# Weights' casts and one head's scaling on GpSimd in the attention steps, and weight loads ordered behind the queries' transfers

## The chip, the core and the metric

The kernel runs on one core of a Trainium2 chip. A core has a matrix engine (TensorE: PE in the profile, with its weight loads shown apart as PEld), VectorE (DVE), ScalarE (ACT), GpSimd (POOL) and SyncE (SP), which here only issues DMAs. The engines run side by side, each through its own list of instructions in a fixed order, and wait for one another by semaphores. The metric is the device time of one execution in microseconds (us); three executions of the kernel before took 1140.64, 1141.03 and 1141.64 us.

## The reference

A two-layer decoder trunk on 512 tokens of width 1024, in float32: a gated mixer, a gated MLP with a short convolution and a gated per-layer embedding in layer 0; then one shared K/V; then, in layer 1, sliding-window attention, and the MLP and embedding again. The change lies in layer 1's attention:

```python
q = (xn @ w_q).reshape(B, nb, BLOCK, N_KV_HEADS, GQA_GROUP, HEAD_DIM)
scores = einsum('bnikgd,bnjkd->bnkgij', q, kblk) * HEAD_DIM ** -0.5
scores = where(valid, scores - slopes * dist, -inf)
m = maximum(max(scores, -1), sink)
e = exp(scores - m)
probs = e / (sum(e, -1) + exp(sink - m))
out = einsum('bnkgij,bnjkd->bnikgd', probs, vblk)
return out.reshape(B, S, N_Q_HEADS * HEAD_DIM) @ w_o
```

There are 16 query heads of 64 in 4 groups, which share a K/V head each, and 4 blocks of 128 tokens; each block sees itself and the block before.

## The kernel before

**Products.** Every float32 operand is split into a high part, rounded to the matrix engine's format `fp32r`, and a remainder. A product is three matmuls: high by high, high by remainder, remainder by high (`mm3`, lines 181 to 183). For a weight the split is done on the way: `load` (line 122) fetches a piece of up to 2048 columns into a raw buffer with one DMA on SP's queue (line 129); `pump` (line 133) takes a unit of up to 1024 columns of it, casts it to the high part `wh` (line 154, on ACT) and subtracts for the remainder `wl` (line 155, on DVE). Four `wh` and four `wl` buffers exist (`WBUFS`). A piece is loaded when its first unit is pumped, so the loops' order is also that of the loads. `chunk` takes the units that a product needs and pumps some ahead.

**The attention steps** (line 864). `steps` holds 16 pairs (group, block), blocks innermost. Turn `i` of the loop calls
- `scores(i)`: eight matmuls of queries by keys (lines 781, 782), and on DVE the choice of the half that is valid (784) and distance, mask and row minimum in one (788); a copy of the sink logits on POOL (774); four exponentials with their sums on ACT (793);
- `fill(i)`: matmuls and casts from the table `beside`, which stand between the attention's own: projections of the queries of groups 1 to 3 (`project`), the first parts of the output projection (`merge`), and `more`, which pumps one unit of weights. `more` stands in steps 0, 1, 3, 4, 6, 7, 10 and 11;
- `mix(i-2)`: probabilities by values (844), and on ACT, DVE and POOL the results' way into the operands of the output projection (848 to 857);
- `turn(i-1)`: four transposes on PE (822), the split of the result (252 on ACT, 253 on DVE), and for blocks with a predecessor two selects on POOL (830);
- `weights(i)`: a reciprocal of the four sums on DVE (801), and each head's probabilities by it: three heads on ACT (805), the first on DVE (807).

In the loop the raw weights have one buffer only (`state["tags"] = [0]`), since the others hold transposed probabilities and values. `queries` (line 641) scales a projection and splits it, and for groups 1 to 3 brings both parts into place with four DMAs on SP's queue (661, 662).

**The order of each engine's list** is made by a planner when the program is built: it goes by the order of the loops, moves `scores`, `turn` and `weights` forward (`tc.high_priority()`), and lets an instruction pass others that are not ready by its own estimates of durations. A change of one instruction's engine can so move others.

The profile names tiles without their numbers: `wraw`, `wh` and `wl` are weights, `sc` scores, `prs` probabilities, `tr` their transposes, `pts` and `u` their split, `pv` values' products, `o` output projection, `oh` and `ol` its operands.

Of the kernel before, what the change touches and what calls it, by code (L numbers as in the profile page):

```python
# [8 lines left out]
F32 = mybir.dt.float32  # L9
# [4 lines left out]
P = 128  # L14
# [34 lines left out]
def tile_yoco(ctx: ExitStack, tc: tile.TileContext, t, out: bass.AP, out_b: bass.AP):  # L49
    nc = tc.nc  # L50
# [14 lines left out]
    pieces, paired = [], set()  # L65
# [51 lines left out]

    units = [(i, q, lo, n) for i, p in enumerate(pieces) for q, (lo, n) in enumerate(p[2])]
    raws, ready = {}, {}
    state = {"raw": 0, "unit": 0, "next": 0, "tags": [0, 1, 2], "turn": 0, "pt": 0}  # L120

    def load(upto, queue=nc.sync):
        while state["raw"] < min(upto, len(pieces)):
            j = state["raw"]
            a, m = pieces[j][:2]
            tags = state["tags"]
            r = wp.tile([P, 2 * UNIT], F32, tag=f"r{tags[state['turn'] % len(tags)]}", bufs=1, name=f"wraw{j}")
            state["turn"] += 1
            queue.dma_start(r[:, :m].rearrange("p (c m) -> p c m", c=2) if j in paired else r[:, :m], a)
            raws[j] = r  # L130
            state["raw"] += 1

    def pump(upto):
        while state["unit"] < min(upto, len(units)):
            i, q, lo, n = units[state["unit"]]
            load(i + 1)
            u = state["unit"]
            own = pieces[i][3]
            if own:
                pool, *tags = own[q]  # L140
                wh, wl = (pool.tile([P, n], F32R, tag=tg, name=f"own{u}_{tg}") for tg in tags)
            else:
                wh = wp.tile([P, UNIT], F32R, tag="wh", bufs=WBUFS, name=f"wh{u}")
                wl = wp.tile([P, UNIT], F32R, tag="wl", bufs=WBUFS, name=f"wl{u}")
            if i in paired:
                whole = raws[i][:, : pieces[i][1]].rearrange("p (c k n) -> p k c n", c=2, n=256)
                src = whole[:, lo // S : (lo + n) // S]
                hi, low = (x[:, :n].rearrange("p (k c n) -> p k c n", c=2, n=256) for x in (wh, wl))
            else:
                src, hi, low = raws[i][:, lo : lo + n], wh[:, :n], wl[:, :n]  # L150
            if u == 0:
                nc.vector.tensor_copy(hi, src)
            else:
                nc.scalar.copy(hi, src)  # L154
            nc.vector.tensor_sub(low, src, hi.bitcast(F32))  # L155
            ready[u] = (wh, wl, n)
            state["unit"] += 1
# [41 lines left out]
    def v(name, i):  # L199
        c = VEC[name] + i  # L200
        return vec[:, c : c + 1]
# [142 lines left out]
    def gain(name, l=0):  # L344
        return lambda k: v(name, l * KD + k)
# [215 lines left out]
    for c in range(4):  # L561
# [4 lines left out]
        for j in range(2):  # L566
            m = 2 * c + j
# [14 lines left out]
            hi = ap.tile([P, S], F32R, tag=f"ah{m}", name=f"ush{m}")  # L582
# [58 lines left out]
    def queries(ps, g, j):  # L641


        qf = tp.tile([P, S], F32, tag="sq", name=f"qf{g}_{j}")
        m = 2 * g + j
        nc.vector.scalar_tensor_tensor(qf, ps, qscale[:, m : m + 1], rstd, op0=ALU.mult, op1=ALU.mult)
        res = [tp.tile([P, S], F32R, tag=("hs", "sg", "c0", "c1")[2 * j + e], name=f"q{g}_{j}_{e}")
               for e in range(2)]
        if g == 0:
            for e, q in enumerate(res):  # L650
                me, it = sides[e], sides[1 - e]
                nc.scalar.copy(q[me, :], qf[me, :])
                nc.vector.tensor_sub(q[it, :], qf[me, :], q[me, :].bitcast(F32))
            return res

        hi = tp.tile([P, S], F32, tag="acc", name=f"qhi{g}_{j}")
        nc.scalar.copy(hi.bitcast(F32R), qf)
        nc.vector.tensor_sub(qf.bitcast(F32R), qf, hi)
        for e, q in enumerate(res):
            me, it = sides[e], sides[1 - e]  # L660
            nc.sync.dma_start(q[me, :].bitcast(F32), hi[me, :])
            nc.sync.dma_start(q[it, :].bitcast(F32), qf[me, :])
        return res

    qs = {0: []}
    for j in range(2):
        qs[0] += queries(qps[j], 0, j)
# [61 lines left out]
    def more():  # L729

        pump(state["unit"] + 1)
# [23 lines left out]
    def fill(i):  # L755
        for f, *args in beside.get(i, []):
            f(*args)
# [9 lines left out]
    def scores(i):  # L767


        g, n = steps[i]  # L770
        nk = 2 * P if n else P
        t0 = (n - 1) * P if n else 0
        pr = prs[:, i % 2]
        nc.gpsimd.tensor_copy(pr[:, :, P], nsink[:, GQ * g : GQ * (g + 1)])
        neg = at.tile([P, GQ], F32, tag="neg", bufs=2, name=f"neg{i}")
        for b in range(2):
            sc = psum(f"sc{i}_{b}").rearrange("p (e h k) -> p e h k", e=2, h=2)
            for j in range(2):
                o = sc[:, j].rearrange("p h k -> p (h k)")[:, :nk]
                q = qs[g][2 * b + j][:, n * P : (n + 1) * P]  # L780
                nc.tensor.matmul(o, q, kh[g // 2][:, g % 2, t0 : t0 + nk], start=True, stop=False)
                nc.tensor.matmul(o, q, kl[g // 2][:, g % 2, t0 : t0 + nk], start=False, stop=True)
            if n:
                nc.vector.copy_predicated(sc[:, :, 0, :], both(own.bitcast(mybir.dt.int32)), sc[:, :, 1, :])
            for j in range(2):
                e = 2 * b + j
                hd = GQ * g + e
                nc.vector.tensor_tensor_reduce(out=pr[:, e, :P], in0=far if n else near, in1=sc[:, j, 0, :],
                                               scale=-slope(hd), scalar=nsink[:, hd : hd + 1],
                                               op0=ALU.add, op1=ALU.min, accum_out=neg[:, e : e + 1])  # L790
        sm = at.tile([P, GQ], F32, tag="sm", bufs=2, name=f"sm{i}")
        for e in range(GQ):
            nc.scalar.activation(pr[:, e, :], pr[:, e, :], AF.Exp, bias=neg[:, e : e + 1], scale=-1.0,
                                 accum_out=sm[:, e : e + 1])
        live[i] = (pr, sm)

    def weights(i):

        pr, sm = live[i]
        ds = at.tile([P, GQ], F32, tag="ds", bufs=2, name=f"ds{i}")  # L800
        nc.vector.reciprocal(ds, sm)
        for e in range(GQ):
            a, r = pr[:, e, :P], ds[:, e : e + 1]
            if e:
                nc.scalar.activation(a, a, AF.Copy, scale=r)
            else:
                nc.vector.tensor_scalar_mul(a, a, r)
        live[i] = pr

    def pair(name):  # L810
# [24 lines left out]
    def mix(i):  # L835
        g, n = steps[i]
        pts = live.pop(i)
        ps = psum(f"pv{i}")
        todo = []
        for b, halves in enumerate(pts):  # L840
            both_halves = (diffs[g][:, n - 1] if b else vt[:, n, g]).rearrange("p a d -> p (a d)")
            todo += [(both_halves, x) for x in halves]
        for j, (lhs, rhs) in enumerate(todo):
            nc.tensor.matmul(ps, lhs, rhs, start=j == 0, stop=j == len(todo) - 1)


        low = side[sides[0], i % 2 * S : (i % 2 + 1) * S]
        nc.scalar.copy(low, ps[sides[1], :])
        o = side[:, 2 * S + i % 2 * N : 2 * S + (i % 2 + 1) * N].rearrange("p (b t) -> p b t", b=2)
        a, low = (x.rearrange("p (b e t) -> p e b t", b=2, e=2) for x in (ps[sides[0], :], low))  # L850
        for e in range(2):
            nc.vector.tensor_add(o[sides[e]], a[:, e], low[:, e])
        cols = slice(n * P, (n + 1) * P)
        for b in range(2):
            oh, ol = o2[2 * g + b]
            nc.scalar.copy(oh[:, cols], o[:, b, :])
            (nc.vector if i == last - 1 else nc.gpsimd).tensor_sub(ol[:, cols], o[:, b, :], oh[:, cols].bitcast(F32))

    last = len(steps)
# [2 lines left out]
    state["tags"] = [0]  # L862
    pts4 = wp.tile([P, 4, S], F32R, tag="r1", bufs=1, name="pts4")
    for i in range(last + 2):
        if i < last:
            with tc.high_priority():
                scores(i)
        if i <= last:
            fill(i)
        if i >= 2:  # L870
            mix(i - 2)
        if i > last:
            fill(i)
        if 0 <= i - 1 < last:
            with tc.high_priority():
                turn(i - 1)
        if i < last:
            with tc.high_priority():
                weights(i)
    state["tags"] = [0, 1, 2]  # L880
    nf = Norm("nf1", [(xp, "x", gain("norm_ffn", 1))])
    for c in range(4):
        for m in (2 * c, 2 * c + 1):
# [226 lines left out]
```

## Time and profile before

| | us |
|---|---|
| median of three executions | 1141.03 |
| the profiled execution | 1141.22 |
| its span, from the first to the last instruction | 1139.5 |
| PE busy | 1127.0 |
| DVE busy | 749.6 |
| ACT busy | 530.0 |
| POOL busy | 107.7 |

The profile is of one execution. Busy time is the time in which an engine had at least one instruction at work; matmuls are pipelined, so a busy PE may still start fewer than it could. The chain that ended last is followed back from the last instruction, each step to what released it. In the timeline a row is start, duration, engine, line, operation, tiles written and read, shapes, count, and in brackets the idle time before it and what ended it. Where a line's instructions are listed, the three durations are shortest, median and longest in ns. Matmuls' granted clock was 0.998 of full speed.

### The profile page before, as it was taken

What the parts mean: (1) busy time and instruction counts of PE and PEld (TensorE: products, weight loads), DVE (VectorE), ACT (ScalarE), POOL (GpSimd) and SP (SyncE); (2) the same over time, 40 slices, a digit from 0 to 9 for tenths busy, and PEclk for the clock granted to TensorE, in tenths of its full rate; (3) what the DMA queues carried; (4) which work ended last, traced back from release to release, by engine and by line L of the source; (5) the groups of instructions that cost most, each with busy time, mean ns of one, the idle gap of its engine ahead of it and who ended that gap; (6) DMA issues with size and microseconds to landing.
All of it is one profiled execution on the core that took longest, in us unless ns stands there. A gap on an engine that the chain in (4) does not pass through costs nothing.

```text
span 1139.5 us, 13604 instructions
## 1 busy us (share of the span) xinstructions
PE 1127.0 (99%) x5266; PEld 940.5 (83%) x5266; DVE 749.6 (66%) x1158; ACT 530.0 (47%) x875; POOL 107.7 (9%) x175
## 2 busy tenths in 40 slices
PE   9999999999999999999999999999999999999997
PEld 7888888888888888888898878888888888888896
DVE  7366477763677367557988977777636763675675
ACT  6533344441344234445657985444313432355562
POOL 2000200000000000021213343000000000000222
PEclk9999999999999999999999999999999999999999
DMA  8422323223223322432224315223223233224302
GB/s 298 145 83 74 111 75 111 101 85 111 78 98 102 111 76 86 134 107 79 74 75 129 93 38 185 98 88 111 78 107 110 66 102 111 93 80 160 111 1 75
DMA packets 25776, 115.41 MB, mean 101 GB/s; under 512 B 2920, under 2 KB 8176, under 8 KB 16240
## 3 DMA queue, kind: packets, MB, share of 16 engines
q1 hardware_dynamic: 25152, 113.89, 29.8%
q8 instruction: 41, 0.67, 0.2%
q10 hardware_dynamic: 560, 0.66, 0.2%
q14 instruction: 23, 0.19, 0.1%
HBM read 108.24 MB, written 2.11 MB: 97 GB/s over the span
## 4 chain that ended last, share of the span: by engine, by line
PE 95%; DVE 2%; issue 1%; ACT 1%; DMA 1%; POOL 0%; SPq 0%; POOLq 0%; DVEq 0%; ACTq 0%
PE up L181 14%; PE up L183 14%; PE up L182 14%; PE d L183 8%; PE d L181 8%; PE d L182 8%; PE gate L181 2%; PE gate L183 2%; PE gate L182 2%; PE u L182 1%; PE u L183 1%; PE u L181 1%; PE o L182 1%; PE o L181 1%; PE o L183 1%; PE q L181 1%
## 5 line engine op out<-in xcount | busy, mean ns | idle before, releaser
L154 ACT CAST wh<-wraw 128x1024 fp32r<-128x1024 f32 (+2 forms) x197 | 202.0, 1028 | 264.6 <-PE d L182 131.0
L155 DVE TENSOR_TENSOR wl<-wraw,wh 128x1024 fp32r<-128x1024 f32 (+1 forms) x198 | 238.4, 1205 | 127.9 <-ACT wh L154 127.6
L181 PE MATMUL up<-nf00h,wh 128*128 128x512 f32 x352 | 137.1, 390 | 0.0
L181 PE MATMUL up<-nf10h,wh 128*128 128x512 f32 x352 | 137.0, 389 | 0.0
L182 PE MATMUL up<-nf00l,wh 128*128 128x512 f32 x352 | 136.9, 389 | 0.0
L183 PE MATMUL up<-nf00h,wl 128*128 128x512 f32 x352 | 136.9, 389 | 0.0
L183 PE MATMUL up<-nf10h,wl 128*128 128x512 f32 x352 | 136.9, 389 | 0.0
L182 PE MATMUL up<-nf10l,wh 128*128 128x512 f32 x352 | 136.9, 389 | 0.0
L181 PE MATMUL d<-ah,wh 128*128 128x512 f32 x352 | 136.9, 389 | 0.0
L182 PE MATMUL d<-al,wh 128*128 128x512 f32 x352 | 136.9, 389 | 0.0
L183 PE MATMUL d<-ah,wl 128*128 128x512 f32 x352 | 136.9, 389 | 0.0
L379 ACT ACTIVATE c<-hs,vec 128x512 f32<-128x512 f32 x88 | 71.5, 815 | 72.0 <-DVE hs L375 71.2
L380 DVE SCALAR_TENSOR_TENSOR c<-hs,vec,c 128x511 f32<-128x511 f32 x88 | 65.8, 749 | 34.5 <-ACT c L379 34.4
L355 DVE TENSOR_TENSOR h<-h,d 128x512 f32<-128x512 f32 x56 | 38.4, 686 | 73.8 <-PE d L183 73.8
L252 ACT CAST ah<-a 128x512 fp32r<-128x512 f32 x44 | 27.4, 622 | 109.5 <-DVE a L385 109.4
L183 PEld LDWEIGHTS up<-nf10h,wl 128*128 128x128 f32 x352 | 66.1, 188 | 13.8
L182 PEld LDWEIGHTS d<-al,wh 128*128 128x128 f32 x352 | 66.1, 188 | 13.8
L183 PEld LDWEIGHTS up<-nf00h,wl 128*128 128x128 f32 x352 | 66.1, 188 | 13.8
L183 PEld LDWEIGHTS d<-ah,wl 128*128 128x128 f32 x352 | 66.1, 188 | 13.7
L182 PEld LDWEIGHTS up<-nf00l,wh 128*128 128x128 f32 x352 | 66.1, 188 | 13.7
L182 PEld LDWEIGHTS up<-nf10l,wh 128*128 128x128 f32 x352 | 66.1, 188 | 13.7
L181 PEld LDWEIGHTS d<-ah,wh 128*128 128x128 f32 x352 | 66.1, 188 | 13.6
(454 smaller groups left out, 2061.7 us busy)
## 6 DMA issues: line engine op xcount, KB each, us to landing
wraw<-in_w_up SPq DMA_DIRECT2D x44, 1024.0 KB, 4.8
wraw<-in_w_down SPq DMA_DIRECT2D x16, 896.0 KB, 4.6
wraw<-in_w_down SPq DMA_DIRECT2D x8, 1024.0 KB, 4.8
wraw<-in_w_gate SPq DMA_DIRECT2D x8, 1024.0 KB, 4.8
wraw<-in_w_u SPq DMA_DIRECT2D x4, 1024.0 KB, 5.9
wraw<-in_w_out SPq DMA_DIRECT2D x4, 1024.0 KB, 4.8
wraw<-in_w_q SPq DMA_DIRECT2D x4, 1024.0 KB, 4.9
wraw<-in_w_o SPq DMA_DIRECT2D x4, 1024.0 KB, 4.9
```

Source lines behind the costliest of these rows:

```text
L154: nc.scalar.copy(hi, src)
L155: nc.vector.tensor_sub(low, src, hi.bitcast(F32))
L181: nc.tensor.matmul(ps, wh[:, a:b], xh, start=st, stop=False)
L182: nc.tensor.matmul(ps, wh[:, a:b], xl, start=False, stop=False)
L183: nc.tensor.matmul(ps, wl[:, a:b], xh, start=False, stop=en)
L252: nc.scalar.copy(hi, src)
L355: nc.vector.tensor_add(h[m], h[m], ps)
L379: nc.scalar.activation(c, hs, AF.Identity, bias=v("conv_b", l * 2 * NJ + col), scale=cw[2])
L380: nc.vector.scalar_tensor_tensor(c[:, 1:], hs[:, : S - 1], cw[1], c[:, 1:], op0=ALU.mult, op1=ALU.add)
```

## The change

Three edits, all of which act in the attention steps:
- the engine of the weights' cast becomes a variable; for turns 1 to 14 of the loop (of 0 to 17) it is POOL, else ACT;
- the first head's scaling in `weights` goes from DVE to POOL, as a product with the broadcast reciprocal;
- `queries` remembers its last transfer, and the next load of a weight is ordered behind it. This is an order in SP's list alone, not a wait on a semaphore.

```diff
-    state = {"raw": 0, "unit": 0, "next": 0, "tags": [0, 1, 2], "turn": 0, "pt": 0}
+    state = {"raw": 0, "unit": 0, "next": 0, "tags": [0, 1, 2], "turn": 0, "pt": 0, "sent": None, "cast": nc.scalar.copy}
+
+    def behind(ins, front):
+
+        tc.add_manual_dep(ins.ins, front.ins.name,
+                          mybir.DependencyInfo(mybir.DependencyClass.NoSync, mybir.DependencyReason.DATA),
+                          reason="order")
...
-            queue.dma_start(r[:, :m].rearrange("p (c m) -> p c m", c=2) if j in paired else r[:, :m], a)
+            ins = queue.dma_start(r[:, :m].rearrange("p (c m) -> p c m", c=2) if j in paired else r[:, :m], a)
+            if state["sent"] is not None:
+                behind(ins, state["sent"])
+                state["sent"] = None
...
-                nc.scalar.copy(hi, src)
+                state["cast"](hi, src)
...
-            nc.sync.dma_start(q[it, :].bitcast(F32), qf[me, :])
+            state["sent"] = nc.sync.dma_start(q[it, :].bitcast(F32), qf[me, :])
...
-                nc.vector.tensor_scalar_mul(a, a, r)
+                nc.gpsimd.tensor_mul(a, a, r.to_broadcast([P, P]))
...
     for i in range(last + 2):
+        state["cast"] = nc.gpsimd.tensor_copy if 0 < i < last - 1 else nc.scalar.copy
         if i < last:
...
     state["tags"] = [0, 1, 2]
+    state["cast"] = nc.scalar.copy
```

## The prediction

> **What bounds the kernel now.** I began with the page: engine shares, then the chain of work that ended last.
>
> ```profile
> span 1139.5 us, 13604 instructions
> ...
> PE 1127.0 (99%) x5266; PEld 940.5 (83%) x5266; DVE 749.6 (66%) x1158; ACT 530.0 (47%) x875; POOL 107.7 (9%) x175
> ...
> PE 95%; DVE 2%; issue 1%; ACT 1%; DMA 1%; POOL 0%; SPq 0%; POOLq 0%; DVEq 0%; ACTq 0%
> ```
>
> TensorE holds the end of the program: it is busy 1127.0 of 1139.5 us and makes 95% of the chain. Work that leaves ACT or DVE is worth something only where PE waits for it. So the next view is busy time by stretches, over the attention steps (some 590 to 690 us), the only place that the change touches. The columns are the stretch, its length, and the busy time (with instruction counts) of PE, PEld, DVE, ACT and POOL, then PE's clock.
>
> ```profile
> 610.00:615.00 5.00, 5.00 (x30) 4.30 (x29) 4.14 (x12) 2.64 (x8) 1.28 (x2) 1.00 0.64 126
> ...
> 645.00:676.00 31.00, 27.35 (x148) 21.32 (x147) 27.87 (x105) 28.79 (x102) 13.86 (x30) 1.00 0.18 52
> ```
>
> Early on PE is full and ACT half empty (2.64 of 5 us). From 645 to 676 us it is the other way round: ACT 28.79 and DVE 27.87 of 31 us, PE only 27.35, and POOL less than half. This is the stage in which the change can be worth something, and the 3.65 us in which PE is idle are near its ceiling. The order of time on PE shows the gaps one by one; brackets give the idle time and what ended it.
>
> ```profile
> 649.27 0.39 PE L183 MATMUL o<-oh,wl 128*128 128x512 f32 x1
> 649.50 0.39 PE L844 MATMUL pv<-pts,vt 128*128 128x512 f32 x1
> 650.68 0.41 PE L822 MATMUL tr<-ident,prs 128*128 128x128 f32 x2 [0.80 <-DVE prs L807]
> ...
> 653.74 0.71 PE L844 MATMUL pv<-pts,vt 128*128 128x512 f32 x2
> 654.93 0.53 PE L822 MATMUL tr<-ident,prs 128*128 128x128 f32 x3 [0.48 <-DVE prs L807]
> ...
> 657.60 0.43 PE L844 MATMUL pv<-pts,vt 128*128 128x512 f32 x1
> 658.50 0.55 PE L822 MATMUL tr<-ident,prs 128*128 128x128 f32 x3 [0.47 <-DVE prs L807]
> ...
> 662.11 0.50 PE L182 MATMUL o<-ol,wh 128*128 128x512 f32 x1 [0.71 <-POOL ol L857]
> ```
>
> Matmuls overlap, so a gap costs more than its bracket. Unhindered, one 512-column matmul starts 0.23 us after the last (649.27 to 649.50). From 649.50 to 650.68 there are 1.18 us, so 0.95 are lost; the second gap loses 1.19 - 0.46 = 0.73, the third 0.90 - 0.23 = 0.67: the bracket and some 0.2 each. These **three gaps, 2.35 us, all end with the first head's scaling on DVE**. The chain in order of time says why the first is late:
>
> ```profile
> 641.95 0.99 ACT prs L805 x3
> 642.93 0.95 ACT wh L154
> ...
> 643.90 1.23 DVE wl L155
> ...
> 645.73 0.26 DVE prs L788
> ...
> 650.04 0.51 DVE prs L807
> ```
>
> A weight's cast on ACT and its remainder on DVE stand ahead of the ninth step's softmax: its first row statistics run only at 645.73.
>
> **The change part by part.** *Casts.* Steps 1 to 14 call the extra pump at steps 1, 3, 4, 6, 7, 10 and 11: seven casts go to POOL; that of step 0 and those of the last two output weights stay on ACT.
>
> ```profile
> L154 ACT CAST wh<-wraw x17: 1032/1041/1059, 560.7 to 695.7; 128x1024 fp32r<-128x1024 f32 x17
> ...
> L774 POOL COPY prs<-nsink x16: 184/190/404, 478.3 to 665.0; 128x4 f32<-128x4 f32 x16
> ...
> L687 POOL CAST diff<-vd x12: 232/235/1239, 590.9 to 602.7; 128x64 fp32r<-128x64 f32 x12
> ...
> L830 POOL TENSOR_SCALAR_AFFINE_SELECT u2h<-pts x1: 636/636/636, 619.0 to 619.0; 128x512 fp32r<-128x512 f32 x1
> ...
> L857 POOL TENSOR_TENSOR ol<-side,oh x30: 450/460/1369, 616.5 to 686.6; 128x128 fp32r<-128x128 f32 x30
> ...
> L807 DVE TENSOR_SCALAR prs<-prs,ds x16: 269/396/598, 595.5 to 677.5; 128x128 f32<-128x128 f32 x16
> ```
>
> ACT loses 7 x 1.04 = 7.3 us. No row shows a 1024-wide cast on POOL. Between the copy of 4 and the cast of 64 elements an element costs 0.75 ns, which makes 0.95 us; from the cast of 64 to the select of 512 it is 0.89 ns, which makes 1.09 us. I take 1.09, from the wider row; the far end is 2.7 us, twice the two-input sum of 512 (1.34, below). Per cast that is -0.1 to +1.6 us of latency against ACT. In the early steps it buys nothing, since PE is full there, and costs nothing while the weights lie ready before their matmuls.
>
> What decides is the pair for the second output weight, at 642.9 and 646.88:
>
> ```profile
> 646.88 1.04 ACT L154 CAST wh<-wraw 128x1024 fp32r<-128x1024 f32 x1
> ```
>
> The first, with its 1.23 us remainder, leaves the chain above, the second the exponentials right behind. The softmax of step 9 then comes 0.95 + 1.23 = 2.2 us earlier, 3.2 with the second cast. The gap in front of it is 0.95, so about 2 us of lead are left, and the next two gaps need 0.73 + 0.67 = 1.40. They should close: **-2.35 us**. The remainders stay on DVE and come back later, by the new place of the load (below).
>
> *First head's scaling.* 16 instructions of 0.40 us leave DVE (6.3 us) and come to POOL at 0.46 as a two-input product (7.4 us). POOL then stands near 123 us in all. DVE no longer holds the scaling behind the next step's row statistics; but POOL works in order and is just then busy with these:
>
> ```profile
> 649.58 0.87 POOL L857 TENSOR_TENSOR ol<-side,oh 128x128 fp32r<-128x128 f32 x2
> ...
> 654.07 0.64 POOL L830 TENSOR_SCALAR_AFFINE_SELECT u9l<-pts 128x512 fp32r<-128x512 f32 x1
> ```
>
> Had the product waited for these, it would end at 650.45 + 0.46 = 650.91 and 655.17, not at 650.55 and about 654.8: some 0.4 us later per gap. With 2 us of lead that is hidden; without, it costs up to 1.1 us over three gaps. I take 0. Behind a product that waits for its reciprocal stand POOL's selects and remainders, and behind these the value and output matmuls; they have at most that delay.
>
> *Loads behind transfers.* Each weight load after a `queries` call is now put behind its four transfers on SP. Two loads stood ahead of them:
>
> ```profile
> 589.18 0.33 SPq L129 DMA_DIRECT2D wraw<-in_w_q  x1
> ...
> 605.40 0.70 SPq L662 DMA_DIRECT2D q<-qf  x1
> ...
> 619.57 0.59 SPq L662 DMA_DIRECT2D q<-qf  x1
> ...
> 651.77 1.10 SPq L662 DMA_DIRECT2D q<-qf  x2
> ...
> wraw<-in_w_q SPq DMA_DIRECT2D x2, 1024.0 KB, 5.2
> ...
> 600.29 0.98 ACT L805 ACTIVATE prs<-prs,ds 128x128 f32<-128x128 f32 x3
> ...
> 603.45 0.40 PE L182 MATMUL q<-n11l,wh 128*128 128x512 f32 x1
> ...
> 611.68 0.38 PE L822 MATMUL tr<-ident,prs 128*128 128x128 f32 x2
> ...
> 613.31 0.40 PE L181 MATMUL q<-n11h,wh 128*128 128x512 f32 x1
> ...
> 628.41 0.39 PE L181 MATMUL q<-n11h,wh 128*128 128x512 f32 x1
> ```
>
> The third query weight was issued at 589.18 and would now be issued at 605.40 + 0.70 = 606.1, land at 611.3, be cast by 612.3 and have its remainder by 613.5. Between 603.45 and 611.68 PE starts 36 matmuls at 0.23 us: by the loop's order 23 of the second weight, 12 of the third and one product. So it wants the third weight at 608.7 and its remainder at 609.2: **in the old order PE would stand for 4.3 us**. But the planner sees the load too, and work lies ready: step 1's scaling began at 600.29 and was over at 601.3, its transposes ran at 611.68. Those, the scores beside them and the products behind fill 1.9 us (611.68 to the next projection at 613.31, and the product ahead), and step 2's come next. I take +0.5 us; ends 0 and 4.3. The fourth weight (issued near 620.2 behind the row at 619.57, landed at 625.4, with cast and remainder ready near 628) stays just inside its first use at 628.41. The second output weight, behind the row at 651.77, is issued near 652.9 and lands at 658; its casts and remainders come to lie at 658 to 661.
>
> *Behind 668 us* the same view, cut there, shows the last of the idle time:
>
> ```profile
> 668.00:676.00 8.00, 6.81 (x37) 5.04 (x36) 7.46 (x29) 6.95 (x25) 2.48 (x5) 1.00 0.00 1
> ```
>
> PE is idle for 8.00 - 6.81 = 1.19 us; with 0.2 for each of four gaps 2.0 are lost. They come behind the stretch of output matmuls that opens at 662.11, while softmax waits for scores. A softmax that is ahead of the fill should halve them: -1.0, ends 0 and -2.0. The gap at 662.11 (0.71, with its restart 0.9) I leave as it is.
>
> Sum: -2.35 - 1.0 + 0.5 = -2.85. The profiled execution took 1141.22 us (1.7 outside its span), 0.19 above the median of 1141.03, so the forecast on the median is **1138.2 us**.
>
> **The rivals.** *The late third weight (slower).* PE keeps its order and stands 4.3 us at 608.7, and the fourth weight costs up to 0.6. For it speaks the old order, which ran 12 matmuls of the third weight ahead of transposes that were ready long before; against it, that the planner sees the new place of the load. The late gain of 2.35 is left: 1141.03 + 4.9 - 2.35 = 1143.6. It decides from a stall of some 4.7 us; if the late gaps stay too, 1146.
>
> *POOL gives it back (about no change).* Three things at once: products 0.4 us late, the casts of the second output weight at 658 to 660 ahead of the remainders for which PE waits at 662.11 (+1 to 2 us), and the two engines in each other's way:
>
> ```profile
> 540.94 1.34 POOL L282 TENSOR_TENSOR n1acc<-n1acc,n1sq 128x512 f32<-128x512 f32 x1 [4.06 <-ACT n1sq L277]
> 541.05 2.32 DVE L155 TENSOR_TENSOR wl<-wraw,wh 128x1024 fp32r<-128x1024 f32 x1
> ```
>
> A remainder that met a POOL sum took 2.32 instead of 1.23 us. With seven casts each beside a remainder, 1.1 us apiece is 7.6 us of DVE, of which two fall where DVE is full: +2.2. With one product's 0.4, 1141.03 - 2.85 + 2.6 = 1140.8. [...]
>
> *Nearly all gaps close.* The lead lasts to the end of attention, and the third weight costs nothing: 2.35 + 2.0 + 0.9 at 662.11 makes 1135.8.
>
> *The edits do little.* The planner reorders so that the gaps reappear elsewhere; the time stays near 1141. I count it with POOL's.
>
> **How the numbers follow.** Forecast 0.42 (its own range 1137 to 1139.6; 0.34 faster, 0.08 within), all gaps 0.10, POOL 0.18 (0.14 within, 0.04 slower), late weight 0.30 (0.04 within, 0.26 slower). Less than 0.2%, some 2.3 us, this measurement hardly tells from no change. So faster 0.44, same 0.26, slower 0.30. The range, 1135.5 to 1144.6, goes from all gaps closed to the late weight with 1 us more.
>
> **What would show it.** Right: casts of about 1.1 us on POOL, no cast on ACT between 605 and 660, no gap above 0.3 us at the transposes of steps 9 to 11, PE fuller than 27.35 in the 31 us that correspond. The third weight's load behind 606 and what PE does at 608 to 613 decides the slower rival; remainders of more than 1.5 us beside casts, or transposes that wait for POOL, the other. The forecast is wrong if PE idles before 645 us by more than 2 us, or if the gaps of steps 9 to 15 keep their 5 us.

## The result and the profile after

The changed kernel takes **1149.53 us** (median of four, 1149.11 to 1150.12), beside 1140.98 for the kernel before (1140.64 to 1141.64): the ratio is 1.0075, with a 95% interval of 1.0057 to 1.0092. That is slower by 8.5 us, where 1138.2 was forecast, and outside the range of 1135.5 to 1144.6. (The prediction's own 1146, for a late weight with the late gaps left, lay outside that range as well.) The profiled execution took 1149.87 us. Its page, the lines that answer to those shown of before:

```profile
span 1148.0 us, 13594 instructions
...
PE 1131.2 (99%) x5266; PEld 942.0 (82%) x5266; DVE 746.2 (65%) x1142; ACT 524.3 (46%) x868; POOL 123.3 (11%) x198
...
PE 91%; DVE 3%; DMA 2%; ACT 1%; issue 1%; POOL 1%; SPq 0%; POOLq 0%; DVEq 0%
```

The work moved as intended: ACT has 7 instructions less, DVE 16 less, POOL 23 more. But PE is busy 4 us longer with the same 5266 matmuls, and DMA is now 2% of the chain. Busy time by stretches (the columns are stretch, length, busy PE, PEld, DVE, ACT, POOL, granted clock, share of the DMA engines, GB/s):

```profile
605.00:610.00 5.00, 4.29 (x19) 3.19 (x17) 2.57 (x12) 2.75 (x11) 0.59 (x2) 1.00 0.96 259
610.00:615.00 5.00, 1.99 (x7) 1.33 (x8) 3.13 (x4) 1.66 (x2) 1.04 (x1) 0.96 0.62 164
615.00:620.00 5.00, 5.00 (x23) 4.12 (x22) 0.92 (x2) 0.79 (x2) 0.49 (x1) 0.70 0.00 0
645.00:676.00 31.00, 28.64 (x152) 22.65 (x151) 25.71 (x87) 24.77 (x90) 21.67 (x36) 1.00 0.41 123
651.00:682.00 31.00, 27.39 (x142) 20.66 (x141) 27.09 (x96) 25.41 (x93) 20.27 (x37) 1.00 0.32 94
```

From 610 to 615 us PE runs 7 matmuls instead of 30. From 615 to 620 it is full again, but with 23 matmuls, at a clock of 0.70. The last row is the late stage 6 us on, since all is later by that much by then: ACT has come down from 28.79 to 25.41 us, and PE, at 27.39 beside 27.35, has gained nothing from it. SP's queue and then PE (start, duration, engine, line, operation, tiles, and in brackets the idle time and what ended it) show the first 6 us:

```profile
605.12 1.20 SPq L671 DMA_DIRECT2D q<-qf  x2
606.37 0.58 SPq L135 DMA_DIRECT2D wraw<-in_w_q  x1
...
626.55 0.54 SPq L135 DMA_DIRECT2D wraw<-in_w_q  x1
...
642.53 0.53 SPq L135 DMA_DIRECT2D wraw<-in_w_o  x1
...
662.16 0.54 SPq L135 DMA_DIRECT2D wraw<-in_w_o  x1
```

```profile
608.68 0.39 PE L191 MATMUL q<-n11l,wh 128*128 128x512 f32 x1
608.90 0.39 PE L192 MATMUL q<-n11h,wl 128*128 128x512 f32 x1
612.48 0.50 PE L190 MATMUL q<-n11h,wh 128*128 128x512 f32 x1 [3.19 <-ACT wh L163]
612.82 0.39 PE L191 MATMUL q<-n11l,wh 128*128 128x512 f32 x1
613.74 0.50 PE L192 MATMUL q<-n11h,wl 128*128 128x512 f32 x1 [0.53 <-DVE wl L164]
614.08 0.40 PE L190 MATMUL q<-n11h,wh 128*128 128x512 f32 x1
...
614.92 0.63 PE L190 MATMUL q<-n11h,wh 128*128 128x512 f32 x1
615.34 0.63 PE L191 MATMUL q<-n11l,wh 128*128 128x512 f32 x1
```

The third query weight leaves at 606.37 instead of 589.18, behind the transfers of group 1. PE runs out of the second weight's matmuls at 608.90. From there to 614.08 it starts four matmuls, which is 0.91 us of work in 5.18: **4.27 us lost**, the two restarts (0.34 instead of 0.23 from 612.48 and from 613.74) included. Then matmuls start every 0.42 us instead of every 0.23. The clock by single microseconds:

```profile
613.00:614.00 1.00, 0.47 (x2) 0.26 (x2) 1.00 (x2) 0.00 (x0) 0.00 (x0) 1.00 0.93 207
614.00:615.00 1.00, 1.00 (x5) 0.77 (x5) 0.82 (x1) 0.00 (x0) 0.00 (x0) 0.80 0.59 131
615.00:616.00 1.00, 1.00 (x4) 0.80 (x3) 0.00 (x0) 0.00 (x0) 0.00 (x0) 0.50 0.00 0
616.00:617.00 1.00, 1.00 (x3) 0.76 (x3) 0.00 (x0) 0.00 (x0) 0.00 (x0) 0.50 0.00 0
617.00:618.00 1.00, 1.00 (x4) 0.65 (x3) 0.00 (x0) 0.00 (x0) 0.00 (x0) 0.50 0.00 0
618.00:619.00 1.00, 1.00 (x10) 1.00 (x9) 0.00 (x0) 0.16 (x1) 0.00 (x0) 0.99 0.00 0
```

It is halved for 0.20 / 0.50 = 0.4 us of the second row and 3 us more, 3.4 us in all, and 0.20 + 3 x 0.50 = **1.70 us** of work are lost. In the profile of the kernel before every microsecond from 600 to 712 us stands at 1.00. Stall and clock make 6.0 of the 8.5 us. The rest is late: if each start-to-start time of PE is counted above 0.2275 us for a 512-column matmul, 0.119 for 256 and 0.111 for 128, PE loses 9.0 us from 640 to 712, and 6.8 in the kernel before: 2.2 more. (This count, of the whole order of time on PE, is used below as what PE "loses"; half clocks are in it.) The waits that the forecast named are gone: in the order of time from 640 to 712 us no wait of PE ends with the first head's scaling, where three did before. Others stand in their place, the longest of them for the split of the transposes and for the output projection's operands:

```profile
654.22 0.36 PE L790 MATMUL sc<-kh,q 128*128 128x256 f32 x1 [0.51 <-DVE pts L262]
...
658.46 0.50 PE L853 MATMUL pv<-pts,vt 128*128 128x512 f32 x1 [0.76 <-ACT pts L261]
...
666.58 0.50 PE L190 MATMUL o<-oh,wh 128*128 128x512 f32 x1 [0.45 <-ACT oh L865]
```

### The profile page after: what moved, and what is told of

Read it like the earlier page. It is cut to its first block, busy times and chain, and to the rows that moved or that the text cites. A ratio compares the mean times of both kernels' runs of the same rounds, so it can differ in the third digit from the quotient of the medians.

```text
span 1148.0 us, 13594 instructions
## 1 busy us (share of the span) xinstructions
PE 1131.2 (99%) x5266; PEld 942.0 (82%) x5266; DVE 746.2 (65%) x1142; ACT 524.3 (46%) x868; POOL 123.3 (11%) x198
## 4 chain that ended last, share of the span: by engine, by line
PE 91%; DVE 3%; DMA 2%; ACT 1%; issue 1%; POOL 1%; SPq 0%; POOLq 0%; DVEq 0%
PE up L192 14%; PE up L190 14%; PE up L191 14%; PE d L192 8%; PE d L191 8%; PE d L190 8%; PE gate L190 2%; PE gate L191 2%; PE gate L192 2%; PE u L191 1%; PE u L192 1%; PE u L190 1%; PE o L190 1%; PE o L191 1%; PE o L192 1%
## 5 line engine op out<-in xcount | busy, mean ns | idle before, releaser
L163 ACT CAST wh<-wraw 128x1024 fp32r<-128x1024 f32 (+2 forms) x190 | 194.7, 1028 | 264.9 <-PE d L191 131.0
L190 PEld LDWEIGHTS up<-nf00h,wh 128*128 128x128 f32 x352 | 66.1, 188 | 13.7
```

The source lines that it names most:

```text
L163: state["cast"](hi, src)
L190: nc.tensor.matmul(ps, wh[:, a:b], xh, start=st, stop=False)
```

## The experiments

The ratios are to the kernel before on the same chip, whose median stood at 1141.0 to 1141.5 us there; they are taken over all executions, and so differ a little from the ratio of the medians. "Half clock" says where the profile of that kernel, which is one execution, has microseconds at 0.50 between 600 and 712 us; each such piece costs 1.7 us.

| run | median us | ratio to before, 95% | half clock at |
|---|---|---|---|
| order_only | 1152.04 | 1.0094 (1.0079 to 1.0110) | 613, 664 (twice as long) |
| cast_and_scale | 1144.12 | 1.0031 (1.0021 to 1.0041) | none |
| cast_only | 1144.32 | 1.0028 (1.0018 to 1.0038) | 658 |
| scale_only | 1141.21 | 1.0000 (0.9992 to 1.0009) | none |
| first_load_only | 1149.26 | 1.0074 (1.0061 to 1.0088) | 612 |
| all_but_first_load | 1142.80 | 1.0018 (1.0009 to 1.0027) | none |
| cast_old_order | 1144.27 | 1.0029 (1.0018 to 1.0041) | 658 |
| cast_scale_old_order | 1144.51 | 1.0033 (1.0020 to 1.0045) | 658 |
| late_pair_cast | 1143.62 | 1.0019 (1.0010 to 1.0027) | 659 |
| late_pair_remainder | 1142.38 | 1.0008 (0.9999 to 1.0018) | 672 |
| late_pair_both | 1142.79 | 1.0013 (1.0004 to 1.0022) | 672 |
| third_weight_used_later | 1149.20 | 1.0070 (1.0057 to 1.0082) | 661 |
| late_pair_cast_query_first | 1142.26 | 1.0009 (1.0000 to 1.0018) | 672 |
| late_pair_cast_query_second | 1142.78 | 1.0014 (1.0006 to 1.0023) | none |
| early_casts | 1143.24 | 1.0016 (1.0007 to 1.0024) | none |
| stall_filled | 1150.87 | 1.0086 (1.0072 to 1.0100) | 664 |

**The three edits apart.** Each undoes one or two of them in the changed kernel; the first keeps the order of the loads alone:

```diff
-        state["cast"] = nc.gpsimd.tensor_copy if 0 < i < last - 1 else nc.scalar.copy
+        state["cast"] = nc.scalar.copy
...
-                nc.gpsimd.tensor_mul(a, a, r.to_broadcast([P, P]))
+                nc.vector.tensor_scalar_mul(a, a, r)
```

> The kernel before with the loads ordered behind the queries' transfers, and nothing else. Theory 1 (the order is the price): PE stands at the first use of the third query weight as after the whole change, 3.35 + 0.9 us of gap and 1.7 us of lower clock, 6.0 in all, and the late output weights put casts and remainders among the last steps, 2 to 3 us more; 1147 to 1150. Theory 2 (GpSimd is the price behind 640 us): the first 6.0 us only, near 1147, and gaps behind 640 us not above the 6.4 us of before.

The other three drop the order; the second also puts the scaling back on DVE, the third the casts on ACT:

```diff
-            state["sent"] = nc.sync.dma_start(q[it, :].bitcast(F32), qf[me, :])
+            nc.sync.dma_start(q[it, :].bitcast(F32), qf[me, :])
```

> The whole change without the order of the loads: casts and scaling on GpSimd, loads where the planner puts them. Theory 1: no stall before 645 us, late gaps smaller than before; 1138 to 1141. Theory 2: the late gaps grow by 2 to 3 us through casts, products and selects in one queue on GpSimd; 1143 to 1144.

> Only the seven casts go to GpSimd. Theory 1: 1138 to 1141, since a cast and its place ahead of the exponentials leave ScalarE. Theory 2: a remainder waits for a cast that waits in GpSimd's queue, 1142 to 1144.

> Only the first head's scaling goes to GpSimd. Theory 1: 1140 to 1141.5, as it is 0.4 us late at the gaps of steps 9 to 11 but frees VectorE. Theory 2: 1142 to 1143, since transposes wait for the product behind selects.

The order alone costs 10.7 us, the casts alone 3.0, the scaling nothing. Against the forecast the casts lose, too. The scaling came out as its first theory said; the other three lie above the slower of their theories, order_only by 2.0 us and the two with casts by 0.1 and 0.3. With the order in place the other two edits give 2.2 us back (10.7 beside 8.5 us over the kernel before). That is not shown to be work taken off ACT and DVE: the profile of order_only has two half clocks more than that of the changed kernel, 3.4 us, behind a loss of 1.97 us at 664, and no theory had those.

**One load.** In the kernel before, only the third query weight's load goes behind group 1's first transfers (`sent` keeps each group's last transfer); and the reverse, the whole change with this one load left free:

```diff
+            front = {-2: (1, 0)}.get(j - first_o)
+            if front:
+                behind(ins, sent[front])
```

> The kernel before, with the load of the third query weight alone ordered behind its transfers. Theory 1 (this one load makes the early stall, and a stall also lowers TensorE's granted clock for some us): 4.3 us of gap and 1.5 to 2 us of slower matmuls at 609 to 618, and late gaps as before; 1146.5 to 1148. Rival (the chain catches up, since later weights are then early against it): 1143 to 1144.

```diff
-            state["sent"] = nc.sync.dma_start(q[it, :].bitcast(F32), qf[me, :])
+            ins = nc.sync.dma_start(q[it, :].bitcast(F32), qf[me, :])
+            if g > 1:
+                state["sent"] = ins
```

> The whole change, but the third query weight's load is free to go ahead. Theory 1: the early 6.0 us are gone, the rest of the change stays; 1143 to 1144. Rival (the late gaps grow by as much once the stall no longer gives the softmax time): 1146 to 1149.

One load behind four transfers costs 8.3 us by itself (1149.26 beside 1141.01), and the change without it 1.8; the two do not add up to the 8.5 of the whole change. In the profile of first_load_only PE starts the third weight's first matmul at 612.41, after 3.33 us of idle time, and the half clock follows at once. From 640 to 712 us PE loses 9.1 us there, as in the changed kernel (9.0): with casts and scaling in their old places the one load brings the late loss, too, which theory 1 did not have (it said 1146.5 to 1148).

**Is it the loads' place that makes the casts dear?** Casts on POOL, with and without the scaling, and the output weights' loads where they stood before:

```diff
+            front = {1: (2, 1), 2: (3, 1)}.get(j - first_o)
+            if front:
+                behind(ins, sent[front])
```

> Only the casts on GpSimd, with SP's list as before; TensorE's list is that of the casts alone. Theory 1a: the waits for queries at 637 and 657 us go (1.3 and 1.6 us), 1140 to 1141.5. Rival: 1143.5 to 1144.5.

> Casts and scaling on GpSimd, with the second and third output weight held behind the same transfers as in the kernel before, so that SP's list is that of before. Theory 1a (the 2.9 us of casts and scaling come from loads that stand ahead of the queries' transfers): the waits for queries at 637 us go, 1140 to 1142, and with the forecast relief of the late gaps 1138 to 1140. Rival (GpSimd's queue makes them): 1143.5 to 1144.5 as without this.

No: PE's idle time near 637 us (0.87 us in cast_only, ended by DVE; 1.22 in cast_and_scale, 0.80 of it ended by the queries' transfers) is gone, and the time stays (1144.27 beside 1144.32, and 1144.51 beside 1144.12). What PE loses from 640 to 712 us grows instead, from 8.1 to 9.5 and from 7.7 to 9.7 us; in the second pair 1.7 of that is a half clock. That theory fell.

**The step behind the -2.35.** Only the two casts of the second output weight go to POOL (the first line added), with the old order of the loads kept by the lines shown above; then their remainders instead (the lines with `rem`, casts on ACT); then both:

```diff
-        state["cast"] = nc.gpsimd.tensor_copy if 0 < i < last - 1 else nc.scalar.copy
+        state["cast"] = nc.gpsimd.tensor_copy if i in (10, 11) else nc.scalar.copy
...
+        state["rem"] = nc.gpsimd if i in (10, 11) else nc.vector
...
-            nc.vector.tensor_sub(low, src, hi.bitcast(F32))
+            state["rem"].tensor_sub(low, src, hi.bitcast(F32))
```

> The kernel before, with only the two casts of the second output weight (turns 10 and 11) on POOL and the weight loads in the places they had before. Theory A, the step of the forecast (ACT's cast holds step 9's statistics back): they start 2 us earlier, the three gaps at the transposes after 650 us close, 1138.6 us (-2.35). Theory D (DVE's remainder behind the cast holds them, and that stays on DVE): the statistics start where they did, near 646.0, the gap at 650.7 stays near 1 us, and since PE's list from step 10 on equals that of the kernel with all casts moved, the time is that kernel's: 1144.2 us (1143.5 to 1144.8). Theory C (each of seven casts costs by contention): two of seven, 1141.9.

> The kernel before, with only the two remainders of the second output weight (turns 10 and 11) on POOL; casts on ACT, loads in their old places. A remainder of 1024 columns on POOL should take some 2.7 us (twice the 1.34 us of 512 columns). Theory D (DVE's remainder holds step 9's statistics): these start some 1.2 us earlier than 645.7, the gaps at 650.7, 654.9 and 658.5 lose 1.5 us or more between them, 1139.3 us (1138 to 1140.3). Theory A (ACT's cast holds them): the gaps stay, 1141 within 0.5. Theory L (any new order of PE's list behind step 10 costs, since output matmuls are spent or left over at the wrong place: here 33 stand in one piece at the end): 1142.5 or more, lost behind 665 us.

> The kernel before, with casts and remainders of the second output weight (turns 10 and 11) on POOL, loads in their old places; PE's list is that of the run with the remainders alone. Theory D: within 0.5 us of that run, since ACT's cast was not what held anything. Theory A: 1 to 2 us less than that run, since the cast leaves ACT as well. Should POOL's 3.7 us per unit hold the remainders for which PE waits (the product's low half): 1 to 2 us more than that run.

The order of time on POOL and on DVE in the run with the two casts alone (its lines lie 10 behind those of the kernel before):

```profile
641.90 1.12 POOL L164 CAST wh<-wraw 128x1024 fp32r<-128x1024 f32 x1
```

```profile
641.83 0.28 DVE L817 TENSOR_SCALAR prs<-prs,ds 128x128 f32<-128x128 f32 x1
642.30 0.85 DVE L862 TENSOR_TENSOR side<-pv,side 64x256 f32<-64x256 f32 x2 [0.18 <-ACT side L858]
643.18 1.23 DVE L165 TENSOR_TENSOR wl<-wraw,wh 128x1024 fp32r<-128x1024 f32 x1
...
645.25 0.33 DVE L798 CUSTOM_DVE_ANT_0 prs<-far,sc,nsink 128x128 f32<-128x128 f32 x1
...
647.54 0.75 DVE L656 SCALAR_TENSOR_TENSOR qf<-q,qscale,n1rstd 128x512 f32<-128x512 f32 x1
...
654.71 0.68 DVE L668 TENSOR_TENSOR qf<-qf,qhi 128x512 fp32r<-128x512 f32 x1
```

The cast is done at 643.02, 0.9 us sooner than before, but DVE is busy until 643.15, and the remainder, a mask and a split still stand ahead of the statistics, which start at 645.25 instead of 645.65 (645.73 in the chain). So the lead is **0.4 us, not 2.2 to 3.2**. It closes the first gap: PE loses nothing above 0.25 us from 640 to 653. What comes instead is at the end of the rows: the remainder of the last queries, 3.1 us behind its scaling in the kernel before (647.94 to 651.06), stands 7.2 us behind it. PE then:

```profile
654.61 0.49 PE L832 MATMUL tr<-ident,prs 128*128 128x128 f32 x2 [0.66 <-DVE prs L817]
...
655.87 0.40 PE L854 MATMUL pv<-u9l,diff 128*128 128x512 f32 x1
658.35 0.30 PE L791 MATMUL sc<-kh,q 128*128 128x128 f32 x1 [2.08 <-DMA q<-qf]
```

2.25 us are lost on the transfer of that remainder, and behind it comes a half clock. (The one execution of eleven at a mean clock of 0.999 took 1142.11 us, so most of the 2.3 us that this run costs seems to be the half clock.) None of the theories had that: D's time is met and its reason is only half right (the remainder does stand ahead, but the gap at 650.7 closes).

With the remainders on POOL instead (2.40 us each, beside 1.23 on DVE), and with both there, step 9's scaling starts at 647.88 and 647.91 instead of 649.95. So it was DVE's remainder, with the order around it, that held the softmax; the cast moved as well adds nothing, and the lead of some 2 us that the forecast wanted does arise. In the run with both:

```profile
647.91 0.87 DVE L817 TENSOR_SCALAR prs<-prs,ds 128x128 f32<-128x128 f32 x1
```

```profile
654.25 0.41 PE L832 MATMUL tr<-ident,prs 128*128 128x128 f32 x2 [1.02 <-DVE pts L263]
...
671.96 0.36 PE L791 MATMUL sc<-kh,q 128*128 128x256 f32 x1 [1.78 <-DVE p13l L263]
```

The first and the third gap are gone, the wait between them is longer than before (1.02 us, where 0.48 stood at 654.93), and a long one comes behind. From 640 to 664 us PE loses 2.3 and 2.2 us instead of 4.1; from 664 to 712 it loses 5.8 and 6.2 instead of 2.6, a half clock of 1.7 in each. What the lead wins in its place is more than given back behind it: the kernels are 1.0 and 1.4 us slower than the one before, where theory D had 1139.3 us for the remainders alone and theory L (a loss behind 665 us by the new order of PE's list) 1142.5 or more. This is theory L's picture, with 1142.38 just under its time. POOL is also 4.8 us busier in these runs, so the order is not shown to be the only reason.

**The wait for the last queries.** The run with the two casts, and the queries' remainder ordered on DVE ahead of one of turn 10's two masks (the one of `b == 0`), or of turn 11's:

```diff
+                if i == 10 and b == 0:
+                    behind(ins, box_q[3, 1])
```

> The run with the two casts of the second output weight on POOL, and the last queries' remainder ordered on DVE ahead of turn 10's second mask, so that its transfers leave some 4 us earlier. Theory Q (the wait of 2.1 us for these transfers is the price of the moved casts): no wait for the transfers near 656, and the time goes from 2.3 us above the kernel before to about none: 1141.4 us (1140.7 to 1142.2). Theory M (the lead is given back in the last steps whatever the order): the wait goes, gaps of 1 us or more come up behind 655 us in its place, 1143 or more.

> The same, with the remainder ordered ahead of turn 11's first mask, some 2 us later than in the run beside it and some 2 us earlier than without an order. Theory Q: the wait shrinks to 0.5 us or less, 1141.4 to 1142. Theory M: 1143 or more, by gaps at other places behind 655 us.

The wait goes in both (in the first the remainder runs at 650.98, between two masks at 650.65 and 651.58). What the casts cost falls from 2.3 us to 1.1 and 1.6, not to none. In the first PE loses time elsewhere, 1.68 us before 653.60 and 1.74 before 672.45, with a half clock at 672. Theory Q and theory M both hold in part.

**The earlier casts.** Only turns before the tenth cast on POOL (1, 3, 4, 6 and 7):

```diff
-        state["cast"] = nc.gpsimd.tensor_copy if 0 < i < last - 1 else nc.scalar.copy
+        state["cast"] = nc.gpsimd.tensor_copy if 0 < i < 10 else nc.scalar.copy
```

> The kernel before, with only the five earlier casts (turns 1, 3, 4, 6 and 7) on POOL, loads in their old places. If casts cost nothing while PE is full: no gap before 645 us, and 1141.3 us within 0.5; all casts together then cost what the last two cost. If each costs by contention with DVE or POOL: +1 (the 3.3 of all casts less the 2.3 of the last two), 1142.3. PE's list changes from step 10 on here as well (nine and six output matmuls in one piece), so that a loss that is all behind 655 us speaks for the order and not for the casts.

It costs 2.1 us, more than either theory said. PE loses 0.15 us in all from 600 to 648, and then 8.5, beside 6.7 in the kernel before. So the casts, all done by 628, hold no matmul while they run. What differs is the order that the planner gave: to DVE from 622 us on, to ACT from 628, to PE from 657. Nor is there a price per cast: these five cost 2.1 us, the last two 2.3, and all seven 3.0 to 3.3. That the order is what costs is the likely reading; no run isolates it.

**The stall shortened, and filled.** In the changed kernel, the third weight's first twelve matmuls a turn later; and twelve matmuls whose result is overwritten, ahead of them:

```diff
-        2: [(project, 2, 0, 0, 4)],
-        3: [(project, 2, 0, 4, 8), (more,)],
+        2: [],
+        3: [(project, 2, 0, 0, 4), (project, 2, 0, 4, 8), (more,)],
```

> The changed kernel, with the first twelve matmuls of the third query weight moved from turn 2 to turn 3 in the table of work beside the attention, so that step 1's transposes, step 3's scores and the products beside them come ahead of them in PE's list. Theory S (the loss is the stall that is left when PE has nothing else ahead of the third weight): 1.9 us of the 4.3 us stall are filled, less of the clock is lost, 1147 us (1146.2 to 1147.6). Theory T (the stall is only moved, since the work put ahead is missing later as cover for the softmax): 1149 or more, with new gaps at the transposes of steps 2 to 8. If the clock falls after any stall of 2 us, the matmuls behind it start every 0.4 us again.

```diff
             box["qp"] = psum(f"q{g}_{j}")
+            if (g, j) == (2, 0):
+                for _ in range(12):
+                    nc.tensor.matmul(box["qp"], xq[0][0][:, :P], xq[0][0], start=True, stop=True)
```

> The changed kernel with twelve matmuls of 512 columns without use (their result is overwritten) in front of the third query weight's first matmul: 12 x 0.23 = 2.7 us of dead work where PE stood for 4.3 us. PE's list moves step 1's transposes and step 3's scores in between as well. Theory K (the half clock follows from the idle time): no stall above 1 us and no clock below 1.00 from 605 to 625 us, and the time is that of the kernel before + 2.7 us of dead work + some 2.3 us of late gaps: 1146.0 us (1145 to 1147.5), 2 to 4 us faster than the changed kernel although PE has more to do. Theory T (as in the run with the third weight used later, what is put forward is missing later): the stall and the half clock go from 610, but gaps and a half clock come up behind 650, 1148.5 or more. If the clock falls to 0.50 near 614 without a stall, it isn't the idle time that makes it.

Theory T's time holds in both, and so does theory K's first part: with the stall filled the clock stays at 1.00 from 605 to 625 us. PE in the run with the later use, and in the filled one:

```profile
612.32 0.50 PE L190 MATMUL q<-n11h,wh 128*128 128x512 f32 x1 [1.73 <-ACT wh L163]
...
660.30 0.30 PE L790 MATMUL sc<-kh,q 128*128 128x128 f32 x1 [1.89 <-DMA q<-qf]
...
677.67 0.36 PE L790 MATMUL sc<-kh,q 128*128 128x256 f32 x1 [1.41 <-DVE p13l L262]
...
680.98 0.33 PE L831 MATMUL tr<-ident,prs 128*128 128x128 f32 x1 [1.61 <-POOL prs L816]
```

```profile
609.09 2.88 PE L727 MATMUL q<-n11h 128*128 128x512 f32 x12
...
662.46 0.30 PE L793 MATMUL sc<-kh,q 128*128 128x128 f32 x1 [1.90 <-DMA q<-qf]
...
679.42 0.36 PE L793 MATMUL sc<-kh,q 128*128 128x256 f32 x1 [1.43 <-DVE p13l L262]
...
682.73 0.33 PE L834 MATMUL tr<-ident,prs 128*128 128x128 f32 x1 [1.62 <-POOL prs L819]
```

The stall of 4.3 us falls to 1.9 or vanishes, and with it the half clock at 614. Yet 1149.2 and 1150.9 us are no less than 1149.5: new waits for the queries' transfers, the transposes' remainders and the scaled probabilities come up behind 655 us, with a half clock of their own. From 640 to 712 PE loses 11.7 and 11.4 us, beside 9.0 in the changed kernel. That is not at the transposes of steps 2 to 8, where T had it, but in the stage in which DVE, ACT and POOL are full. A likely reason, not tested by itself: while PE stood, these engines got ahead with the softmax, and without the stall they do not.

## Why the prediction was wrong

- **The third weight's load: the time was right, the step was not.** Issue was forecast at 606.1 (606.37), cast and remainder by 612.3 and 613.5 (612.43 and, at the first matmul that needs it, 613.74), PE's need at 608.7 (609.1 here), the stall of an unchanged order at 4.3 us (4.27). The step that failed is "But the planner sees the load too, and work lies ready ... I take +0.5". PE's list up to step 9 is the same in both kernels, as the profiles show: the second weight's matmuls, twelve of the third, then the transposes. The evidence on record for the old order was the trace; for a new one there was none. What took the place of the +0.5 is a stall of 4.3 us, with 1.7 us of half clock behind it. This was the slower rival, with a chance of 0.30.
- **Its price was too small as well:** 4.9 us, where stall and half clock cost 6.0. No term of the sum had the clock.
- **A load that was overlooked.** "Two loads stood ahead of them" counts the third and the fourth query weight; the first output weight's, at 613.33 before, stood ahead of group 2's transfers too. It is now issued at 642.53. (The fourth query and the second output weight leave behind the transfers that were named, at 626.55 and 662.16, later by what all is later by then. The fourth makes no stall, as said: PE loses 0.1 us from 620 to 640.) So the first output weight's casts and remainders, done by 633.4 before, fall at 647.6 to 653.1, into the full stage, on POOL and on DVE:

```profile
647.61 1.04 POOL L163 CAST wh<-wraw 128x1024 fp32r<-128x1024 f32 x1 [0.30 <-DMA wraw<-in_w_o]
648.59 0.65 POOL L783 COPY prs<-nsink 128x4 f32<-128x4 f32 x1
649.21 1.51 POOL L866 TENSOR_TENSOR ol<-side,oh 128x128 fp32r<-128x128 f32 x1
650.66 1.03 POOL L163 CAST wh<-wraw 128x1024 fp32r<-128x1024 f32 x1
```

```profile
651.73 1.41 DVE L164 TENSOR_TENSOR wl<-wraw,wh 128x1024 fp32r<-128x1024 f32 x1 [1.34 <-POOL wh L163]
...
653.99 0.33 DVE L797 CUSTOM_DVE_ANT_0 prs<-far,sc,nsink 128x128 f32<-128x128 f32 x1
```

  The second cast stands behind a copy and a remainder on POOL, DVE waits 1.34 us for it in order, and step 9's statistics start behind it at 653.99, 8.3 us later than before, where all is some 6 us late. The forecast named casts in POOL's way only for 658 to 660.
- **The three late gaps, -2.35.** "The softmax of step 9 then comes 0.95 + 1.23 = 2.2 us earlier" rests on the second output weight's cast and remainder being gone from there. They did go, with its load; the overlooked load put the first output weight's in their place. Nor would a free way have been enough. With the load in its old place and the casts alone moved, the lead is 0.4 us (late_pair_cast); with both off ACT and DVE it is the 2 us forecast, and there "They should close" holds for two of the three gaps: 1.9 of the 2.35 us are won up to 664 us. The step that failed is that this stays won: 3.5 us are lost behind it. The -1.0 behind 668 us has no support either: every run with a cast on POOL loses more from 664 to 712 us (3.4 or more) than the 2.6 of the kernel before.
- **The scaling at 0** holds: scale_only is at 1.0000. Three transposes there wait for POOL's product (0.95, 0.57 and 0.66 us, up to 650.75, 655.01 and 658.95) as they waited for DVE's before (0.80, 0.48 and 0.47). That is 0.4 us more in all, where 1.1 was the far end; the wait near 662 shrinks from 0.71 to 0.22, so that the sum stays: the 0 is in part luck.
- **Durations:** the cast was taken at 1.09 us; three of the rows above show 1.03 to 1.12; of the seven in the changed kernel six take 1.03 to 1.04 and one 2.07. The product, taken at 0.46, averages 0.40 there and 0.46 in scale_only. DVE's 178 remainders of 1024 columns take 221.4 us together, 219.5 in scale_only and 220.3 in the kernel before: what the POOL rival put at 7.6 us is 1.9 at most. A remainder of 1024 columns took about twice as long on POOL (2.40 us in late_pair_remainder, beside 1.23 on DVE); the scaling of 128 did not, as a product with a broadcast factor (0.40 to 0.46 beside DVE's 0.41 by a scalar).

Shown is that the one load makes the stall, and that casts on POOL cost 1 to 3 us in the kernels that the planner then makes. That the new order of the lists is the reason is argued, not shown, and which entry of them costs it is open. Casts on POOL with PE's and DVE's old lists were not tried.

## What to carry to other kernels

A load ordered behind a transfer is late by arithmetic, and the arithmetic held to 0.4 us; believe it, and take work that fills the hole only from a list that shows it there. Before a stage is credited with a lead, follow every engine that the waiting row needs: taking the cast off ACT freed 1 us of an engine, and DVE, next in the same chain, let 0.4 of it through. Then ask what the stages behind do with the lead: where DVE was freed as well, 2 us arrived, and PE lost more than that again later. And where TensorE lost 2.0 us or more in one place, its clock fell as well each time here, eight times of eight, and about 1.7 us more were lost: look at the clock behind a stall, and expect what is filled in one place to come back in another while the engines behind stay full.

## What the runs showed of the hardware

**The half clock.** I had not expected it. In these 18 kernels' profiles from 600 to 712 us the granted clock falls to 0.50 for 3.4 us at a time (in order_only near 664 for twice that), 1.7 us lost each; never in the kernel before, whose longest loss in one place is 0.98 us. It came behind each of the eight single losses of 2.0 us or more, behind five of the fourteen between 1.5 and 2.0, and in none of the runs whose longest was 1.4 or less. Moving the idle time moved it, and filling the stall took it away from there. One kernel's executions split by it: late_pair_cast_query_second took 1141.77 to 1142.34 us in three executions at a mean clock of 0.999, 1142.69 to 1143.58 in seven at 0.997, and 1144.42 in one at 0.995, and one such piece is 1.7 of 1140 us, 0.0015 of the mean clock. Losses of 1.6 to 2.3 us in one place were enough in ten of the thirteen places; why nine others between 1.5 and 2.0 us had no half clock behind them, no run shows.
